# Hybrid decoder trunk: split PSUM tiles, paired chunks and postponed steps in the mixers

## The chip, the cores and the metric

The kernel runs on one core of a Trainium2 chip. The metric is the device time of one execution, in microseconds (us), lower is better. The core has TensorE (PE; PEld are its weight loads), VectorE (DVE), ScalarE (ACT), GpSimd (POOL) and SyncE (SP), which issues the DMAs. Each engine runs its own instructions in the order of the program.

## The reference

One step of a two-layer trunk over 1024 prompt tokens and 32 sample tokens (8 sequences of 4), width 1024, fp32. Cut to what matters:

```python
# layer 0: S5 state space mixer (32 groups of 16 channels, 64 complex states) and retention (4 heads of 128)
bb = f * b                                   # complex product per group: the input matrices of the S5
bu = einsum('blgh,gph->blgp', u, bb);  s = associative_scan(a, bu);  y = Re(c s) + d u
scores = einsum('bihd,bjhd->bhij', q, k) * decay                 # retention, chunk by chunk
o = scores @ v + (q * q_dec) @ s;   s = gamma**c * s + (k * k_dec).T @ v
# layer 1: HGRN2 (8 heads of 128)
scores = where(causal, (q exp(b)) (k exp(-b)).T, 0);  o = scores @ v + (q exp(b)) @ s
s = exp(b_last) * s + (k exp(b_last - b)).T @ v
# both: per-head RMSNorm * silu(gate), output projection, residual, then a gated MLP with a width-3 conv
```

## The kernel before

Activations lie with features on the 128 partitions and tokens along the free axis, cut into three token chunks `CH` of 384, 384 and 288. A dense tile (`dense`, `mm`, `mm1`, L258) multiplies a 1024x128 weight tile with all tokens: for each chunk 8 row blocks times 3 passes (weight and activation are both split into a high and a low fp32r part), 72 matmuls, into one of 4 `acc` PSUM banks. VectorE then empties the bank. The other 4 PSUM banks are the ring `misc`, for all small products of the mixers.

The order of all instructions is made while the program is built. `run_jobs` walks through the dense tiles. `at(dt, fn)` puts a side step on a list with a due time; `tick` moves the clock on by 1/8 after each row block, so that one unit is one token chunk of a dense tile and three units are a tile, and `run_side` emits every side step that has come due. An instruction of a side step thus stands at a fixed place between the matmuls of the dense tiles, whether or not its inputs are there by then: where they are not, TensorE waits in front of it. `flush` emits all that is left. Due times come from the table `P`.

The parts that the change touches:

- Start of layer 0 (`first`): the first two weight tiles run while the S5's constants are worked out on VectorE (`s5_setup`, `s5_inputs`, replayed at L150), then `rms1` puts the logarithms of the mean squares on ScalarE (L338, L340), `finish` puts the exponentials (L348) on it and `rms3`, `rms4` on VectorE (L351 to L355).
- S5 inputs (`s5_x`): for each of 16 pairs of groups, `bst` makes two small input matrices on VectorE (L818 to L821: two products and a sum each, from the tile `bc`, loaded by a DMA for each 4 groups), GpSimd multiplies them with powers (`va`, L843 to L847), TensorE transposes the result (`turn`, L856) and multiplies it with the tokens (`prod`, L865). `s5_within` and `s5_carry` scan over time on VectorE (L880 to L884). `s5_y` makes the outputs; it calls `bst` again for each pair (L818, L819, L823, L824).
- Retention (`retention`): 8 chunks of 128 tokens a head. `first(n)` puts a score product and a transpose into one `misc` bank; VectorE takes the score (`sT`, L1149), ScalarE the transpose (`kt`, L1150), GpSimd makes `qd`. `second(n)`, due `lagA` later, puts the state product (L1161), the output product (L1162) and the product with the old state (L1164) into one bank; VectorE makes the new state `S` (L1169) and ScalarE copies the output (L1170).
- HGRN2 (`hgrn`): per head and token chunk a chain on VectorE (`prep`, `scans`, `base`, `level` three times; L1553 to L1609), its last product `kfin` on GpSimd (L1613). Then for each of 8 chunks `first(nn)` (scores L1652, transpose L1653, products of the levels L1636, all in one bank; ScalarE copies the levels into `sTb`, L1642 and L1645; VectorE adds the diagonal blocks by a predicated copy, L1657; ScalarE copies `kt`, L1659) and `second(nn)` (L1670, L1671, L1673; VectorE `S`, L1676 or L1678; ScalarE the output, L1679).

In both layers a head takes three dense tiles (q, k or f, v), in layer 1 four from the sixth head on (a gate tile), so its side steps lie beside the tiles of the next head.

## Time and profile before

| | us |
|---|---|
| median of 3 runs | 2786.41 (2781.28 to 2787.82) |
| profiled execution, its time | 2786.47 |
| profiled execution, its span | 2784.5 |
| PE busy | 2632.7 (95%) |
| DVE busy | 1623.1 (58%) |
| ACT busy | 978.2 (35%) |
| POOL busy | 780.9 (28%) |

The span goes from the first to the last instruction. Busy shares over the whole span mix stages with different limits; a table by stretch and the list of waits say more. In such a table "PEclk" is the clock granted to TensorE as a share of full speed; in a list of waits a line reads "who waits <- for whom: us in total, times, longest".

### The profile page before, as it was taken

The numbers are of one execution on the slowest core, as the hardware profiler recorded it, in microseconds if no ns is written. First come the engines' busy times: TensorE is split into PE (matmuls) and PEld (weight loads), VectorE is DVE, ScalarE is ACT, GpSimd is POOL, SyncE is SP. The second block draws the span as 40 slices with busy tenths as digits, with TensorE's granted clock in tenths as the row PEclk, the third lists the DMA queues.
The fourth block names the chain that finished last, engine by engine and source line by source line (L and its number), as shares of the span: only waits on it lengthen the run. The fifth ranks groups of instructions, "written<-read, shape, count | busy, mean of one in ns | idle before, by whom it ended". The sixth has DMA issues, their size and how long they took to land.

```text
span 2784.5 us, 42698 instructions
## 1 busy us (share of the span) xinstructions
PE 2632.7 (95%) x16388; PEld 2598.3 (93%) x16388; DVE 1623.1 (58%) x3414; ACT 978.2 (35%) x2120; POOL 780.9 (28%) x1173
## 2 busy tenths in 40 slices
PE   6778998999999999999989999989999999999998
PEld 5768998999999999999988889989999999999998
DVE  8996664565444444445787787765455444444445
ACT  4224444452212121214444445444432222222224
POOL 5636671321101010102434344442211010101013
PEclk8899999999999999999999999999999999999999
DMA  3412224111111111112211111112211111111112
GB/s 120 99 42 64 67 78 136 42 49 46 50 42 50 42 50 42 50 42 76 76 50 47 40 56 47 47 40 77 78 48 46 46 46 46 46 46 46 46 46 88
DMA packets 110539, 159.96 MB, mean 57 GB/s; under 512 B 18944, under 2 KB 48256, under 8 KB 110336
## 3 DMA queue, kind: packets, MB, share of 16 engines
q1 hardware_dynamic: 109760, 156.65, 17.9%
q8 instruction: 129, 2.11, 0.3%
q14 instruction: 74, 0.61, 0.1%
q10 hardware_dynamic: 576, 0.59, 0.1%
HBM read 136.45 MB, written 20.74 MB: 56 GB/s over the span
## 4 chain that ended last, share of the span: by engine, by line
PE 77%; DVE 15%; ACT 3%; issue 2%; POOL 1%; DMA 1%; SPq 1%; DVEq 0%; ACTq 0%; POOLq 0%
PE acc L258 71%; DVE hF L1606 1%; DVE s_t L881 1%; PE misc L1113 1%; DVE s_t L880 1%; DVE s_t L882 1%; DVE rb L351 1%; PE misc L1673 1%; DVE hS L1607 1%; DVE sall L884 0%; DVE lv L1601 0%; DVE sall L883 0%; DVE nsq L355 0%; DVE hR L1580 0%; DMA x<-in_x_dram 0%
## 5 line engine op out<-in xcount | busy, mean ns | idle before, releaser
L258 PE MATMUL acc<-hh,whi 128*128 128x384 f32 (+1 forms) x3320 | 1111.4, 335 | 9.2 <-ACT hh L284 7.0
L258 PE MATMUL acc<-hl,whi 128*128 128x384 f32 (+1 forms) x3320 | 1085.2, 327 | 8.8 <-DVE hl L290 8.8
L258 PE MATMUL acc<-hh,wlo 128*128 128x384 f32 (+1 forms) x3320 | 1084.4, 327 | 0.4 <-POOL wlo L189 0.4
L258 PEld LDWEIGHTS acc<-hl,whi 128*128 128x128 f32 x3320 | 635.8, 192 | 13.6 <-DVE hl L290 11.8
L258 PEld LDWEIGHTS acc<-hh,whi 128*128 128x128 f32 x3320 | 636.7, 192 | 11.0 <-ACT hh L284 7.8
L258 PEld LDWEIGHTS acc<-hh,wlo 128*128 128x128 f32 x3320 | 634.1, 191 | 1.0 <-POOL wlo L189 0.7
L1306 POOL TENSOR_TENSOR sl<-cv,rstd 128x384 f32<-128x384 f32 x132 | 122.0, 924 | 1218.4 <-ACT cv L345 1218.4
L188 ACT ACTIVATE whi<-raw 128x512 fp32r<-128x512 f32 x392 | 239.3, 620 | 394.1 <-PE acc L258 385.4
L189 DVE TENSOR_TENSOR wlo<-raw,whi 128x512 fp32r<-128x512 f32 x298 | 238.9, 802 | 143.9 <-ACT whi L188 141.1
L258 PE MATMUL acc<-hdl,whi 128*128 128x384 f32 (+1 forms) x984 | 318.2, 323 | 0.0
L258 PE MATMUL acc<-hdh,wlo 128*128 128x384 f32 (+1 forms) x984 | 318.2, 323 | 0.0
L258 PE MATMUL acc<-hdh,whi 128*128 128x384 f32 (+1 forms) x984 | 317.8, 323 | 0.0
L1335 DVE TENSOR_TENSOR x<-acc,x 128x384 f32<-128x384 f32 (+1 forms) x264 | 138.3, 524 | 239.4 <-PE acc L258 239.1
L258 PE MATMUL acc<-ys,whi 128*128 128x384 f32 (+1 forms) x768 | 187.8, 330 | 9.8 <-DVE x L617 3.7
L1298 ACT ACTIVATE cv<-ext,vec 128x384 f32<-128x384 f32 x132 | 90.6, 687 | 288.1 <-DVE ext L1286 226.8
L258 PEld LDWEIGHTS acc<-hdh,whi 128*128 128x128 f32 x984 | 185.1, 188 | 0.3
L258 PEld LDWEIGHTS acc<-hdl,whi 128*128 128x128 f32 x984 | 185.1, 188 | 0.3
L258 PEld LDWEIGHTS acc<-hdh,wlo 128*128 128x128 f32 x984 | 185.3, 188 | 0.0
L189 POOL TENSOR_TENSOR wlo<-raw,whi 128x512 fp32r<-128x512 f32 x94 | 127.5, 1358 | 203.7 <-ACT whi L188 202.9
L1300 DVE SCALAR_TENSOR_TENSOR cv<-ext,vec,cv 128x384 f32<-128x384 f32 x132 | 78.0, 591 | 169.2 <-ACT cv L1298 169.2
L282 ACT ACTIVATE hdh<-sl 128x384 fp32r<-128x384 f32 x132 | 65.9, 499 | 247.8 <-DVE sl L1323 247.8
L258 PEld LDWEIGHTS acc<-ys,whi 128*128 128x128 f32 x768 | 136.8, 192 | 12.8 <-DVE x L617 4.0
(379 smaller groups left out, 3636.6 us busy)
## 6 DMA issues: line engine op xcount, KB each, us to landing
raw<-in_w_gate_dram SPq DMA_DIRECT2D x88, 256.0 KB, 2.6
raw<-in_w_up_dram SPq DMA_DIRECT2D x88, 256.0 KB, 2.6
raw<-in_w_dn_dram SPq DMA_DIRECT2D x88, 256.0 KB, 2.6
raw<-in_w_c_dram SPq DMA_DIRECT2D x64, 256.0 KB, 2.7
raw<-in_w_ab_dram SPq DMA_DIRECT2D x40, 256.0 KB, 2.8
x<-in_x_dram SPq DMA_DIRECT2D x15, 528.0 KB, 7.2
ush<-uD SPq DMA_DIRECT2D x128, 34.0 KB, 1.9
xD<-x SPq DMA_DIRECT2D x8, 528.0 KB, 3.2
```

What stands on the lines that cost most here:

```text
L188: nc.scalar.activation(hi[:, s], raw, AF.Copy)
L189: eng.tensor_tensor(lo[:, s], raw, hi[:, s].bitcast(F32), OP.subtract)
L258: self.nc.tensor.matmul(ps[:, :c1 - c0], a[:, o:o + 128], b[:, c0:c1], start=first and p == 0, stop=last and p == 2)
L282: nc.scalar.activation(h, src, AF.Copy)
L351: self.nc.vector.scalar_tensor_tensor(b, b, -0.5, a, OP.mult, OP.mult)
L880: eng.tensor_tensor(t2[hi], s[lo], ms[lo].to_broadcast(half), OP.mult)
L881: eng.tensor_tensor(t2[lo], s[hi], ms[hi].to_broadcast(half), OP.mult)
L882: (eng2 or eng).tensor_tensor(t1, s, mr.to_broadcast(shape), OP.mult)
L1298: nc.scalar.activation(cv[:, :ln], ext[:, 0:ln], AF.Identity, bias=self.v(f"cb{l}", m), scale=cwv(0, m))
L1300: nc.vector.scalar_tensor_tensor(cv[:, :ln], ext[:, 1:ln + 1], cwv(1, m), cv[:, :ln], OP.mult, OP.add)
L1306: nc.gpsimd.tensor_tensor(s[:, :npr], cv[:, :npr], self.rstd[:, c0:c0 + npr], OP.mult)
L1335: nc.vector.tensor_tensor(X[m][:, c0:c1], ps, X[m][:, c0:c1], OP.add)
```

## The change

1. **Separate PSUM tiles.** A `first` now takes two `misc` banks: one that only VectorE reads (scores) and one that only ScalarE reads (transposes, level products). `second` is cut in two: `states` (state products, one bank, VectorE) and `outputs` (one bank, due `lagO` = 0.5 or `lagP` = 0.4 units after).
2. **Chunks in pairs.** One such step serves two chunks: 4 pairs a head in retention, 5 groups of 2 or 1 in HGRN2. In retention the decay matrix is replaced by a row factor (`kinv`) and a triangle in one VectorE instruction, the query decay is put on the output (by VectorE, with the copy out of PSUM), and `qd` on GpSimd goes. In HGRN2 the predicated copy becomes a step of its own (`inner`, due `mid` = 0.25 after).
3. **S5 input matrices at once.** `s5_b`, called once in `first` of layer 0 right after the constants, makes all 32 matrices `b1` by 9 VectorE instructions and their turned copies `b2` by 6 ScalarE instructions, from three DMAs that `s5_load` issues. `bst` goes; in `s5_y` a broadcast copy by ScalarE takes its place. `bc` is loaded for `s5_y` only, at half the size.
4. **Postponed steps.** While the program is built a model (`Ahead`) follows when each engine would finish each instruction and when each tile is ready. `at` takes a list of needed tiles (`need`), a condition (`ok`) and a class (`thr`). A step that is due is held back while its inputs, or the next `misc` bank, are ready by the model more than `slack` = 100 ns later than TensorE (for `inner`: VectorE) would get to it, and so are the later steps of its class. `at` drops all three in phase "A", so it holds from the start of layer 1 on. `require` emits what a tile must have before it may start: in phase "C" a head's q and v tiles wait until the head two before is done, a gate tile until its norm is. `flush` and `require` do not ask the model. At most 3 token chunks of HGRN2 are live (`live`).

The core of the diff (waits and names as in the text; the same `need`/`ok` lists are given to the other steps of the mixers):

```diff
+    def at(self, dt, fn, need=None, ok=None, thr=None):
         self.seq += 1
+        if self.ph == "A":
+            need = ok = thr = None
+        self.side.append([(self.now if self.base is None else self.base) + dt, self.seq, fn, need, ok, thr, False])
...
+    def step(self, until):
+        barred = set()
+        for i, x in enumerate(self.side):
+            t, _, fn, need, ok, thr, _ = x
+            if until is not None and t > until:
+                return False
+            if thr in barred or (ok is not None and not ok()) or (
+                    until is not None and need is not None and self.late(need())):
+                if thr is not None:
+                    barred.add(thr)
+                x[6] = True
+                continue
+            self.side.pop(i)
+            self.base = max(t, self.now) if x[6] else t
+            fn()
+            self.base = None
+            return True
+        return False
+    def late(self, need):
+        ...
+        t = max([a.ready(*need, eng=eng)] + [a.over_with(n) for n in a.ring.get(self.misc_key, [])[:banks]])
+        return t > a.at[eng] + P["slack"]
+    def require(self, done):
+        while self.ph == "C" and not done():
+            assert self.step(None)
...
             play(len(setup))
+            self.s5_b()
             u_work(0)
...
+    def s5_b(self):
+        for g, n in ((0, 12), (12, 12), (24, 8)):
+            ...
+            nc.vector.tensor_tensor(a, B[:, 0], self.fr[:, G, None].to_broadcast([128, n, SH]), OP.mult)
+            nc.vector.tensor_tensor(b, B[:, 1], self.fis[:, G, None].to_broadcast([128, n, SH]), OP.mult)
+            nc.vector.tensor_tensor(self.b1[:, G], a, b, OP.add)
+            nc.scalar.activation(self.b2[0:64, G], self.b1[64:128, G], AF.Copy, scale=-1.0)
+            nc.scalar.activation(self.b2[64:128, G], self.b1[0:64, G], AF.Copy)
...
-            self.bst(bc, g, 2, b1, self.fr, self.fis, False)
-            self.bst(bc, g, 2, b2, self.frs, self.nfi, True)
...
-            self.bst(bc, g, 2, bz3[:, :, 16:144], self.fr, self.fis, False)
+            nc.scalar.activation(bz3[:, :, 16:144].rearrange("p g (r h) -> p g r h", h=2 * SH)[:, :, :, 0:SH],
+                                 self.b1[:, g:g + 2, None, :].to_broadcast([128, 2, 4, SH]), AF.Copy)
...
+        def first(p):                                            # retention
+            ps, pt = self.misc(), self.misc()
+            ...  # two score products into ps, two transposes into pt
+            nc.scalar.activation(kt, by(pt[:, :256]), AF.Copy, scale=self.c("kdec", h))
+            nc.vector.scalar_tensor_tensor(sT, by(ps[:, :256]), self.c("kinv", h),
+                                           self.tri[:, None, :].to_broadcast([128, 2, 128]), OP.mult, OP.mult)
+        def states(p):
+            pk = self.misc()
+            ...  # two state products into pk, then two updates of S on VectorE
+        def outputs(p):
+            po = self.misc()
+            ...  # per chunk the output product and the product with the old state
+            nc.vector.tensor_tensor(by(o[:, 256 * p:256 * p + 256]), by(po[:, :256]),
+                                    qdec[:, None, :].to_broadcast([128, 2, 128]), OP.mult)
...
+        PAIRS = ((0, 0, 2), (0, 2, 1), (1, 0, 2), (1, 2, 1), (2, 0, 2))        # HGRN2
+        def first(g):
+            ps, pt = self.misc(), self.misc()
+            ...  # scores into ps; transposes and level products into pt; ScalarE copies levels and kt
+            def inner():
+                for x in range(m):
+                    V.copy_predicated(sT[:, x], self.mdiag, ps[:, 128 * x:128 * x + 128])
+            self.at(P["mid"], inner, lambda: ("vector", [sT[:, :m]]), None, "rec0")
...
         def qtile(w, R):
+            self.qheads.append(R)
+            self.require(lambda: len(self.qheads) < 3 or self.qheads[-3].get("smp") and self.qheads[-3].get("sec") == 8)
```

## Rows read from the trace of the kernel before

**Rows 1.** Stretches: length, busy PE PEld DVE ACT POOL, PEclk, DMA, GB/s.
```profile
66.00:200.00 134.00, 97.03 (x549) 92.88 (x550) 126.61 (x370) 30.74 (x76) 65.46 (x118) 0.86 0.29 70
200.00:430.00 230.00, 209.85 (x1421) 204.67 (x1420) 153.81 (x387) 105.87 (x276) 148.47 (x239) 0.97 0.24 67
...
1372.00:1672.00 300.00, 271.93 (x1780) 264.73 (x1779) 238.76 (x571) 141.05 (x403) 119.00 (x115) 0.94 0.14 48
1672.00:1870.00 198.00, 177.58 (x1148) 173.27 (x1147) 138.74 (x324) 95.33 (x260) 85.79 (x83) 0.96 0.14 45
...
1950.00:2740.00 790.00, 790.00 (x4899) 789.08 (x4898) 372.75 (x662) 216.71 (x394) 114.80 (x235) 1.00 0.16 50
```

**Rows 2.** Waits of TensorE over the whole span.
```profile
PE misc L1670 <- ACT kt L1659: 27.3, 11, 4.6
PE misc L856 <- POOL va L847: 25.8, 6, 10.1
PE misc L1673 <- DVE S L1676: 16.0, 6, 3.2
PE misc L1161 <- ACT kt L1150: 9.8, 4, 2.7
PE misc L1053 <- DVE vf L1046: 9.1, 3, 4.2
...
PE misc L1164 <- DVE S L1169: 8.7, 6, 3.9
```

**Rows 3.** Waits of all engines, 1372 to 1880 us.
```profile
ACT kt L1659 <- DVE sTb L1657: 81.9, 58, 5.0
DVE sTb L1657 <- ACT sTb L1645: 53.2, 24, 5.3
ACT hy L1679 <- DVE S L1678: 52.8, 30, 4.4
```

**Rows 4.** Instructions in order of time around 1508 us: start, length, engine.
```profile
1508.18 0.29 DVE L1657 COPY_PREDICATED sTb<-mdiag,misc 128x128 f32<-128x128 uint8 x1
...
1508.50 0.28 ACT L1659 ACTIVATE kt<-misc 128x128 f32<-128x128 f32 x1 [4.04 <-DVE sTb L1657]
...
1508.83 0.38 PE L1670 MATMUL misc<-vt,kt 128*128 128x128 f32 x1 [2.37 <-ACT kt L1659]
```

**Rows 5.** Busy time by stretch, one head of layer 1.
```profile
1494.00:1553.30 59.30, 52.37 (x346) 50.95 (x346) 47.74 (x114) 28.98 (x83) 24.29 (x24) 0.94 0.14 46
```

**Rows 6.** Busy time of the instructions that touch the tile `ba` (DVE; L818, L821, L823, L824).
```profile
66.00:160.00 94.00, 14.98 (x64) 0.84 0.38 90
200.00:430.00 230.00, 18.84 (x48) 0.97 0.24 67
```

**Rows 7.** Busy time of the instructions of L819.
```profile
66.00:160.00 94.00, 6.84 (x32) 0.84 0.38 90
200.00:430.00 230.00, 4.02 (x16) 0.97 0.24 67
```

**Rows 8.** Waits of all engines, 66 to 200 us.
```profile
POOL va L843 <- DVE b L821: 24.9, 11, 5.5
```

**Rows 9.** Instructions in order of time at the start, three places.
```profile
50.63 0.58 ACT L338 ACTIVATE sacc<-misc,eps 128x384 f32<-128x384 f32 x1 [4.30 <-PE misc L334]
...
54.31 1.30 ACT L348 ACTIVATE sacc<-sacc 128x384 f32<-128x384 f32 x3
...
57.80 0.18 DVE L150 COPY s_frs<-s_fr 64x32 f32<-64x32 f32 x1
...
58.01 0.56 DVE L351 SCALAR_TENSOR_TENSOR rb<-rb,sacc 128x384 f32<-128x384 f32 x1
...
70.62 0.47 PE L856 MATMUL misc<-ident,va 128*128 128x128 f32 x1 [10.09 <-POOL va L847]
```

**Rows 10.** Groups of instructions, 0 to 500 us: count, busy us, mean ns, idle before.
```profile
L1149 DVE TENSOR_TENSOR sT<-misc,dq 128x128 f32<-128x128 f32 x32 | 9.1, 283 | 3.3 <-PE misc L1146 2.9 <-PE misc L1162 0.2
...
L1170 ACT ACTIVATE yr<-misc 128x128 f32<-128x128 f32 x32 | 8.8, 276 | 38.8 <-DVE S L1169 35.9 <-DVE S L1167 2.8
```

662 lines of the change are left out of this document (454 added, 208 removed).

## The prediction

> **What bounds the kernel now.** I read the busy times by stretch first [rows 1]. In the MLPs TensorE is busy all the time at full clock: 790.00 of 790.00 us in the second one. There nothing changes and nothing can be won. The time that can be won lies where TensorE stands still, or runs at the lower of its two clock levels (1.2 against 2.4 GHz) after having stood still. For a stretch I count its idle time plus (1 - PEclk) times its length. That gives 37.0 + 18.8 = 55.8 us for 66 to 200 (S5 inputs and scans), 20.2 + 6.9 = 27.1 us for 200 to 430 (retention, S5 outputs), 28.1 + 18.0 = 46.1 us for 1372 to 1672 (HGRN2, five heads) and 20.4 + 7.9 = 28.3 us for 1672 to 1870 (its other heads). The reader should see that VectorE is busy 94% from 66 to 200 and 80% from 1372 to 1672, but 67% and 70% in the other two.
>
> Then the list of waits says in front of what TensorE stands [rows 2]. In layer 1: for `kt` 27.3 us and for `S` 16.0 us. In layer 0: for `va` 25.8, `kt` 9.8, `S` 8.7 us, and most of 9.1 for `vf`. Behind these stand waits between ScalarE and VectorE [rows 3]: `kt` waits 81.9 us for the predicated copy, the predicated copy 53.2 us for the level copies, the output copy 52.8 us for `S`. `kt` needs nothing from the predicated copy; both only read the same PSUM bank. One such stall in order of time [rows 4]: VectorE gets to its copy at 1508.18, since its queue is full; `kt` starts at 1508.50, after 4.04 us of idle ScalarE; TensorE goes on at 1508.83, after 2.37 us.
>
> **Layer 1, from 1372 to 1870.** Split banks let `kt` run when its transposes are there, and postponed steps keep TensorE from standing in front of what the model calls late. Neither takes work away: VectorE keeps its 47.74 us a head [rows 5]. TensorE's own floor for that head is 59.30 less 6.93 idle less 0.06 x 59.30 = 48.8 us. Two queues of nearly the same length won't overlap perfectly. I take 53 us a head (VectorE 90% busy) against 60 (300 us are five heads): 5 x 7 = 35. The bounds are 58 (what is late merely moves) and the floor, where all 46.1 us come back. From 1672 to 1870 VectorE has room, and I take two thirds of 28.3: 19; bounds 9 and 28.3. Against it stands `require`. From the third head on, a q tile waits until the head two before is done, and whatever is left is emitted at one place without asking the model. Behind it in TensorE's queue stands the whole next tile. No row shows this wait. It costs nothing if the head is done, and a third of a head's VectorE work, 16 us, if one token chunk is still open. I take 1 us for each of six heads, -6, since a head's steps were due before that point even now. Sum: 48, from about 7 to 74.
>
> **S5 inputs, 66 to 200.** `bst` goes: 14.98 + 6.84 = 21.8 us of VectorE up to 160 [rows 6, 7], an upper bound, as neighbours overlap a little. GpSimd stands 24.9 us for its results [rows 8], and TensorE for `va` behind it. With VectorE at 94% I count three quarters as reaching TensorE: 16, bounds 5 and 22. What is late next is VectorE's scan itself, and the DMA that brings the tokens.
>
> `s5_b` brings back 9 products at about 0.283 us [rows 10], 2.5 us of VectorE, and a new wait at a bad place. Its 6 ScalarE copies stand ahead of the logarithms in ScalarE's queue and wait for VectorE's constants, which are done at 58 us [rows 9]. The logarithms started at 50.63 and can now start at 57.8 + 2.5 + 0.3, about 61. The exponentials started 3.7 us after them and would end their first at about 65.2, so that `rms3` starts there and not at 58.01: 7 us later, and with it the scaling of the tokens, their stores and `va`. TensorE stood until 70.62 for `va`, of which some 2 to 3 us were the wait for `bst` (24.9 us in 11 waits), now gone. I take -5, bounds 0 and -10. The three DMAs of `s5_load` go into SP's queue ahead of later weights; I count nothing, as the first `va` is the later one; if that cover fails, it is inside the same bound.
>
> **Retention and S5 outputs, 200 to 430.** ScalarE no longer waits for VectorE in front of `kt`: of 9.8 us I take back 9. For `S` I take 4 of 8.7: fewer waits, but two updates now run in a row half a unit ahead of the outputs. TensorE's clock gives 3. The 18.84 + 4.02 = 22.9 us that `bst` costs VectorE there [rows 6, 7] are what keeps its queue short. They pay for the output copies that move to VectorE: 16 at most twice 0.283 us each, 9.1 us, against 8.8 us that ScalarE loses [rows 10]. `qd` on GpSimd goes and hides behind other work; ScalarE's broadcast copy for `s5_y` too, as ScalarE is 46% busy. Phase "A" drops all conditions, so due times stay what they were, and a step that comes early still stops TensorE. Sum 16, bounds 4 and 22.
>
> At one place a rule speaks against the change. One copy of 128 columns takes ScalarE 0.276 us and a VectorE instruction 0.283 us [rows 10]; in a pair, what the first chunk's product waits for is done later by one such piece. The Trainium skill (Perfetto Trace Analysis, Optimizing Scalar/DVE Operations) says that where these engines are not saturated but cause bubbles on others, smaller instructions may let work be done sooner. By that rule pairing is the wrong way round; it is a rival below.
>
> **Sum.** 48 + 16 - 5 + 16 = 75 us off the profiled execution's 2786.5 us (its span of 2784.5 and 2 around it): 2711 us. That execution is 0.1 us from the median of the runs, so no correction is made. About 0.3%, or 8 us, can be told from no change.
>
> **The rivals.**
> - *VectorE takes over as the bound of layer 1.* Its order is fixed too, and a faster TensorE only moves the wait to the `acc` banks, which VectorE empties. For it: 47.74 against 48.8 us [rows 5]. Against it: VectorE's own 53.2 us of waiting [rows 3] mostly go. With 57 us a head, 10 us after that, 2 us for each `require` and 10 less in layer 0: 15 + 10 - 12 + 17 = 30 off, 2756 us.
> - *All of it comes back.* 74 in layer 1, 42 in layer 0 (20 + 22): 2670 us. Against it: the start, and the equal queues.
> - *Pairs lengthen the chain.* 40 full pairs (24 in HGRN2, 16 in retention) times 0.276 + 0.283 us [rows 10], if nothing hides it: 22 us less gain, 2733 us. For it: due times don't move with the pairs. Against it: in layer 1 the postponing covers it.
> - *It does not do what it says.* The model's clock and the chip's drift apart, steps are held or let go at the wrong places, and the waits come back under other names; with the late start and VectorE's gain of layer 0 about even: 2784 us.
> - *Slower: `require` emits chains in one piece.* If a held step leaves one token chunk open at each of six q tiles, TensorE stands 16 us [rows 5] each: 96 us, against 54 + 27 won, 15 us slower, 2801 us; with more left, beyond. It decides from 13.5 us a head (81 / 6). For it: postponing delays the end of each head, and classes hold back what stands behind. Against it: VectorE's work fits into a head's time.
>
> **How the numbers follow.** Forecast 0.47 (own range 2690 to 2732), pairs 0.10, VectorE 0.18, all of it 0.08, no effect 0.07, slower 0.10. The likeliest gives 2711 us. From 2670 (all bounds at their best) to 2772 (the VectorE case at its worse end) lie the forecast, the pairs, nearly all of the VectorE case and half of the best one, about 0.78. Faster by over 0.3%: 0.47 + 0.10 + 0.18 + 0.08 = 0.83; within 0.3%: 0.07; slower: 0.10.
>
> **What would show it.** Layer 1: the wait of TensorE for `kt` and `S` gone from the list, heads of about 53 us, PEclk there at 0.97 or more; if heads take 57 or more and TensorE waits in front of `acc`, VectorE bounds. Start: the logarithms at about 61 us, the first transpose of `va` near 75; no later wait for `bst`'s successor. Retention: `kt` starts without waiting for `sT`. The prediction is wrong if layer 1 keeps over 50 us of idle and slow time, if q tiles start after long gaps, or if the start costs over 10 us.

## The result and the profile after

The changed kernel takes 2764.4 us (median of 2761.6 to 2769.1) against 2786.7 us before (2781.3 to 2787.8): ratio 0.9926, 95% interval 0.9907 to 0.9945. 22 us came off where 75 were forecast. The sign was right. The time lies in the wide range (2670 to 2772), outside the forecast's own (2690 to 2732) and nearest to the rival in which VectorE takes over (2756). Less than a third of the gain came, and the runs below show that even these 22 us are not made of what the forecast made them of.

The busy times by stretch of the changed kernel come first (length, busy PE, PEld, DVE, ACT, POOL, PEclk, DMA, GB/s); the first four answer to [rows 1], the fifth is one head of HGRN2 and answers to [rows 5], the last is a piece of the scans in layer 0.

```profile
66.00:200.00 134.00, 98.76 (x567) 95.54 (x568) 126.08 (x300) 31.65 (x75) 72.70 (x121) 0.85 0.27 69
200.00:430.00 230.00, 216.03 (x1467) 211.28 (x1465) 140.75 (x310) 102.71 (x250) 136.28 (x212) 0.97 0.26 72
1372.00:1672.00 300.00, 278.96 (x1826) 269.05 (x1826) 245.47 (x577) 148.41 (x392) 123.82 (x119) 0.98 0.15 48
1672.00:1870.00 198.00, 185.11 (x1192) 179.00 (x1191) 136.30 (x316) 98.75 (x243) 80.81 (x79) 0.97 0.15 48
1485.20:1541.05 55.85, 51.28 (x346) 49.54 (x345) 47.21 (x113) 28.23 (x76) 22.75 (x23) 1.00 0.15 49
154.20:177.30 23.10, 18.29 (x109) 17.93 (x110) 22.09 (x56) 5.98 (x14) 3.75 (x3) 0.85 0.05 13
```

From 1372 to 1672 TensorE stands still 21.0 us instead of 28.1, at PEclk 0.98 instead of 0.94: better, but far from what was forecast. From the first `hq` (the evacuated q) of the third head to that of the sixth, three heads, it takes 172.4 us (1426.51 to 1598.87), before 180.0 (1441.60 to 1621.63): 57.5 us a head instead of 60.0, where I had forecast 53. The fifth line is the useful one: at full clock TensorE is busy for 51.28 us in a head.

The waits of TensorE in layer 1 (1330 to 1890) answer to [rows 2]; in this trace nearly every instruction carries line L208, so they are told apart by tile:

```profile
PE misc L208 <- ACT kt L208: 7.4, 8, 2.1
PE acc L208 <- ACT whi L208: 7.3, 6, 2.1
PE acc L208 <- POOL wlo L208: 7.2, 7, 2.5
PE misc L208 <- DVE S L208: 5.5, 7, 1.7
```

`kt` (27.3) and `S` (16.0) have shrunk as forecast. In their place stand `whi` and `wlo`, the two halves of a converted weight, which before cost TensorE 1.3 us in all of layer 1. How they come about is seen around 1503 us (instructions of four engines in order of time: start, length, in brackets the idle time before):

```profile
1502.58 0.55 DVE L208 TENSOR_TENSOR hz<-acc,rstd 128x384 f32<-128x384 f32 x1
1503.17 0.53 ACT L208 ACTIVATE hz<-hz 128x384 f32<-128x384 f32 x1 [6.64 <-DVE hz L208]
1503.60 0.62 ACT L208 ACTIVATE whi<-raw 128x512 fp32r<-128x512 f32 x1
1504.29 1.42 POOL L208 TENSOR_TENSOR wlo<-raw,whi 128x512 fp32r<-128x512 f32 x1 [0.68 <-ACT whi L208]
...
1505.76 0.44 PE L208 MATMUL acc<-hh,wlo 128*128 128x384 f32 x1 [0.64 <-POOL wlo L208]
```

VectorE is late with the evacuation `hz`. ScalarE stands 6.64 us for it, since the sigmoid is next in its fixed order. The weight conversion stands behind the sigmoid, GpSimd's half behind that, and TensorE at the end of the row. Two groups of waits say how much of it there is, the first from 1372 to 1672, the second from 1672 to 1872; first before, then changed:

```profile
ACT hz L345 <- DVE hz L1469: 6.3, 9, 0.8
...
ACT gt L345 <- DVE gt L1247: 3.0, 6, 1.1
```

```profile
ACT hz L208 <- DVE hz L208: 37.3, 9, 9.1
ACT gt L208 <- DVE gt L208: 45.3, 13, 8.5
```

The 81.9 us that ScalarE stood for the predicated copy [rows 3] are gone, but it now stands for VectorE at these two places, 82.6 us.

To see which stage gained, I take three landmarks in each trace: the first `hq` of layer 1 (all of layer 0 lies ahead of it), the last `ys<-hy` (HGRN2 lies between the two), and the end. After the last `ys` all kernels need 866 to 869 us. In the table "to HGRN2" is the first landmark and "HGRN2" the difference of the two.

| kernel | us | ratio to before (95%) | to HGRN2 | HGRN2 |
|---|---|---|---|---|
| before | 2786.7 | | 1357.4 | 561.1 |
| changed | 2764.4 | 0.9926 (0.9907 to 0.9945) | 1346.6 | 546.7 |
| f3: before + input matrices at once | 2768.9 | 0.9937 (0.9921 to 0.9952) | 1340.5 | 560.9 |
| f1: before + banks apart | 2785.6 | 0.9993 (0.9983 to 1.0003) | 1363.3 | 554.2 |
| g1: f1 with five banks | 2790.7 | 1.0016 (1.0006 to 1.0025) | 1360.9 | 560.7 |
| e1: changed, no holding | 2779.9 | 0.9977 (0.9967 to 0.9987) | 1349.1 | 567.0 |
| g5: e1 with single chunks | 2771.3 | 0.9946 (0.9931 to 0.9960) | 1344.8 | 557.4 |
| e5: changed, retention's banks shared | 2761.5 | 0.9909 (0.9894 to 0.9924) | 1340.9 | 550.2 |
| f2: changed, HGRN2's banks shared | 2747.1 | 0.9856 (0.9839 to 0.9872) | 1345.4 | 531.8 |
| e2: changed, sigmoid and silu later | 2751.4 | 0.9880 (0.9865 to 0.9895) | 1347.5 | 534.9 |
| e7: changed, 1 us of margin | 2748.2 | 0.9860 (0.9845 to 0.9875) | 1344.2 | 535.5 |
| e3: changed, no reciprocals | 2743.7 | 0.9851 (0.9833 to 0.9868) | 1344.6 | 528.4 |
| e4: changed, copies behind the logarithms | 2760.9 | 0.9911 (0.9896 to 0.9926) | 1338.5 | 550.1 |
| e6: changed, S a step of its own | 2766.7 | 0.9927 (0.9912 to 0.9941) | 1345.4 | 551.9 |
| e8: changed, outputs later | 2758.9 | 0.9900 (0.9883 to 0.9916) | 1346.5 | 542.8 |
| c4: e2, e4, e7, e8 together | 2760.3 | 0.9902 (0.9884 to 0.9920) | 1339.6 | 553.7 |
| g4: c4 with three hq | 2765.2 | 0.9922 (0.9906 to 0.9939) | 1339.4 | 557.6 |
| c5: e5, f2, e4 together | 2745.9 | 0.9855 (0.9840 to 0.9869) | 1336.5 | 539.4 |
| c7: c5 + e2 | 2729.2 | 0.9804 (0.9787 to 0.9820) | 1339.3 | 523.5 |
| c8: c5 + conversions earlier | 2746.1 | 0.9864 (0.9849 to 0.9879) | 1335.8 | 541.3 |

The landmarks are of one profiled execution each, so the table itself says how far to trust them. Eight kernels have layer 0 exactly as changed (changed, e1, e2, e3, e6, e7, f2, g5): 1344.2 to 1349.1. Four have HGRN2's code as changed (changed, e4, e5, e8): 542.8 to 550.2. In these four the order is nevertheless not the same, as the model that postpones steps begins layer 1 with other clocks: of 941 VectorE instructions in e8's HGRN2, 825 stand in the order of the changed kernel. In e4 it is 928 of 941, and yet HGRN2 took 3.4 us longer there, so the order is not all of this scatter. A profiled execution can also lie off the median of its kernel, e1's by 4.3 us (2784.2). So under 5 us in layer 0 and under 8 us in HGRN2 I read nothing into a single kernel.

### The profile page after: what moved, and what is told of

It reads as the page before. It is cut to its first block, busy times and chain, and to the rows that moved or that the text cites. A ratio compares the mean times of both kernels' runs of the same rounds, so it can differ in the third digit from the quotient of the medians.

```text
span 2761.6 us, 42451 instructions
## 1 busy us (share of the span) xinstructions
PE 2631.6 (95%) x16388; PEld 2593.2 (94%) x16388; DVE 1603.2 (58%) x3261; ACT 971.7 (35%) x2048; POOL 767.3 (28%) x1144
## 4 chain that ended last, share of the span: by engine, by line
PE 74%; DVE 17%; ACT 3%; issue 2%; DMA 1%; SPq 1%; POOL 1%; DVEq 0%; ACTq 0%; POOLq 0%
PE acc L208 69%; PE misc L208 5%; DVE s_t L208 2%; DVE hR L208 2%; DVE hF L208 1%; DVE hS L208 1%; DVE rb L208 1%; DVE sall L208 1%; DVE lv L208 1%; SPq L208 1%; DVE nsq L208 1%; DVE hy L208 1%; ACT sTb L208 1%; DMA x<-in_x_dram 0%; DVE hl L208 0%
## 5 line engine op out<-in xcount | busy, mean ns | idle before, releaser
L208 PE MATMUL acc<-hh,whi 128*128 128x384 f32 (+1 forms) x3320 | 1101.9, 332 | 16.2 <-ACT hh L208 6.4
L208 PE MATMUL acc<-hl,whi 128*128 128x384 f32 (+1 forms) x3320 | 1081.9, 326 | 8.1 <-DVE hl L208 8.1
L208 PE MATMUL acc<-hh,wlo 128*128 128x384 f32 (+1 forms) x3320 | 1081.5, 326 | 8.0 <-POOL wlo L208 7.2
L208 PEld LDWEIGHTS acc<-hh,whi 128*128 128x128 f32 x3320 | 630.7, 190 | 20.6 <-ACT whi L208 7.7
L208 PEld LDWEIGHTS acc<-hl,whi 128*128 128x128 f32 x3320 | 630.5, 190 | 12.7 <-DVE hl L208 10.8
L208 PEld LDWEIGHTS acc<-hh,wlo 128*128 128x128 f32 x3320 | 629.7, 190 | 10.9 <-POOL wlo L208 9.5
L208 POOL TENSOR_TENSOR sl<-cv,rstd 128x384 f32<-128x384 f32 (+2 forms) x176 | 151.0, 868 | 1219.8 <-ACT cv L208 1219.8
L208 ACT ACTIVATE whi<-raw 128x512 fp32r<-128x512 f32 x392 | 239.0, 620 | 398.1 <-PE acc L208 386.5
L208 DVE TENSOR_TENSOR x<-acc,x 128x384 f32<-128x384 f32 (+1 forms) x360 | 187.6, 523 | 281.1 <-PE acc L208 280.8
L208 DVE TENSOR_TENSOR wlo<-raw,whi 128x512 fp32r<-128x512 f32 x298 | 238.7, 801 | 140.7 <-ACT whi L208 137.8
L208 PE MATMUL acc<-hdl,whi 128*128 128x384 f32 (+1 forms) x984 | 317.9, 323 | 0.0
L208 PE MATMUL acc<-hdh,wlo 128*128 128x384 f32 (+1 forms) x984 | 317.7, 323 | 0.0
L208 PE MATMUL acc<-hdh,whi 128*128 128x384 f32 (+1 forms) x984 | 317.4, 323 | 0.0
L208 DVE SCALAR_TENSOR_TENSOR cv<-ext,vec,cv 128x384 f32<-128x384 f32 (+1 forms) x264 | 156.0, 591 | 173.1 <-ACT cv L208 168.4
L208 PE MATMUL acc<-ys,whi 128*128 128x384 f32 (+1 forms) x768 | 189.7, 333 | 12.5 <-DVE x L208 4.8
L208 ACT ACTIVATE cv<-ext,vec 128x384 f32<-128x384 f32 x132 | 90.7, 687 | 287.9 <-DVE ext L208 226.7
L208 PEld LDWEIGHTS acc<-hdl,whi 128*128 128x128 f32 x984 | 184.9, 188 | 0.3
L208 PEld LDWEIGHTS acc<-hdh,whi 128*128 128x128 f32 x984 | 184.8, 188 | 0.3
L208 PEld LDWEIGHTS acc<-hdh,wlo 128*128 128x128 f32 x984 | 185.0, 188 | 0.0
L208 POOL TENSOR_TENSOR wlo<-raw,whi 128x512 fp32r<-128x512 f32 x98 | 134.0, 1370 | 171.9 <-ACT whi L208 151.0
L208 ACT ACTIVATE hdh<-sl 128x384 fp32r<-128x384 f32 x132 | 65.9, 499 | 249.3 <-DVE sl L208 249.3
L208 PEld LDWEIGHTS acc<-ys,whi 128*128 128x128 f32 x768 | 138.0, 193 | 15.8 <-DVE x L208 5.1
```

The lines of the kernel that those rows point to most:

```text
L208: return fn(*a, **k)
```

## The experiments

### What each part of the change is worth

**f3_inputs_only.** `s5_b`, `s5_load`, the smaller `bc` and ScalarE's broadcast copy, put into the kernel before; nothing else.

```diff
-            self.bst(bc, g, 2, b1, self.fr, self.fis, False)
-            self.bst(bc, g, 2, b2, self.frs, self.nfi, True)
+            (once, ahead of u_work:) self.s5_b()
```

> The kernel before, with one part of the change alone: the state space mixer's input matrices made at once (with the copies for the outputs on ScalarE). Theory (this part is what gained in layer 0: 7.5 us up to the first v tile, and 2 to 4 more in the state space mixer's outputs): about 2776 us (2773 to 2780). Rival (the pairs in retention carry half of layer 0's gain of 11): 2779 to 2784 us, no more than 7.5 off.

Measured: 2768.9 us, 16.6 off, more than either expected. Its first `vf` comes at 154.16 (before 161.71), its last `sT` at 384.98 (401.88), its first `hq` at 1340.5. So the input matrices gain 7.5 us up to the first v tile and 9.4 more in the stretch of retention and the state space mixer's outputs. It is alone worth three quarters of the whole change.

**f1_split_only.** Only the separate banks, in the kernel before.

```diff
-            ps = self.misc()
+            ps, pt = self.misc(), self.misc()
-            nc.tensor.transpose(ps[:, 128:256], k[:, c], self.ident)
+            nc.tensor.transpose(pt[:, 128:256], k[:, c], self.ident)
(and p0 beside p1 in HGRN2)
```

> The kernel before, with one part of the change alone: in retention and in HGRN2 the scores that VectorE reads get a bank of their own beside the transposes and level products that ScalarE reads. No pairs, no postponing, no other S5 inputs. The prediction's step (kt's waits, 27.3 + 9.8 us and more, go and the time comes back): about 2762 us (2755 to 2770). Theory by now (kt came late because VectorE's queue is late; without its bank TensorE goes on and stands for S or sTb of the same queue instead): 2783 us (2778 to 2788), with kt's waits under 8 us and those for S and sTb longer by 20 us or more.

Measured: 2785.6 us, no change. The waits for `kt` went, as the prediction said. The first fence has two of TensorE's stalls in retention in the kernel before, the second the same two places in f1:

```profile
193.74 0.49 PE L1161 MATMUL misc<-vt,kt 128*128 128x128 f32 x2 [2.09 <-ACT kt L1150]
...
206.65 0.49 PE L1161 MATMUL misc<-vt,kt 128*128 128x128 f32 x2 [2.61 <-ACT kt L1150]
```

```profile
192.55 0.49 PE L1161 MATMUL misc<-vt,kt 128*128 128x128 f32 x2 [2.13 <-DVE sT L1149]
...
205.36 0.76 PE L1161 MATMUL misc<-vt,kt 128*128 128x128 f32 x2 [2.51 <-DVE sT L1149]
```

Same instruction, same place, same length, another name. This product doesn't read `sT` at all. It may be waiting for the PSUM bank that VectorE has yet to empty, as each chunk now takes one more of the four banks in the ring `misc`. That would make it a question of banks, which the next run asks.

**g1_split_5banks.** f1 with one bank moved from the projections to `misc`.

```diff
-ACC = 4
+ACC = 3
```

> The kernel before with the scores in a bank of their own, as in f1_split_only, and the eight PSUM banks divided 3 to 5 instead of 4 to 4 between the projections' sums and everything else. Theory (the split brought nothing because each chunk now takes one more of four banks, and TensorE stands in front of a bank that VectorE has not emptied: the waits for sT at the state products, for vt at the scores, 10 us between 184 and 441 and 18 us in layer 1): half of these go, about 2772 us (2766 to 2778). Rival (the order of work behind VectorE sets the pace, banks or not; or three banks are too few for the projections): 2781 to 2795 us.

Measured: 2790.7 us; the theory of the bank ring falls. TensorE's waits in retention (184 to 441):

```profile
PE misc L1162 <- DVE sT L1149: 6.5, 3, 2.5
PE misc L1164 <- DVE S L1169: 6.0, 4, 3.9
...
PE misc L1161 <- DVE sT L1149: 0.8, 1, 0.8
```

With a fifth bank the state product (L1161) goes, and the very next product (L1162), which does read `sT`, stands there for it. VectorE is late at that place whatever bank it reads; `kt` was only the first to show it. In layer 1 the names changed likewise: from f1 to g1 TensorE's waits for `vt` fall from 10.5 to 3.0 us and those for `kt` rise from 1.5 to 7.7. (The projections pay too: one wait of 6.5 us in front of `hq` with three banks, 2.3 with four. That a gain of a few us hides behind this is not ruled out.) The Trainium skill (Perfetto Trace Analysis, Matmuls) advises to rotate independent matmul groups through different banks so that evacuation overlaps; here neither one bank more per chunk nor a fifth bank gained, since the groups are not independent of VectorE for longer than one product.

**e1_no_hold.** The changed kernel without postponing.

```diff
-        return t > a.at[eng] + P["slack"]
+        return False
```

> The changed kernel, but no step is ever held back because the model says that its operands are late: every step is emitted at its due time, the conditions on earlier steps stay. Theory (postponing is what shortened layer 1): TensorE again stands in front of what is late, some 10 of the 14 to 16 us that layer 1 gained are lost, about 2775 us (2770 to 2781), with TensorE's waits for S, kt and sTb back by that much between 1330 and 1750. Rival (the separate banks and the pairs shortened it, postponing only moves waits about): 2764 us give or take 4.

Measured: 2779.9 us. Postponing is worth 15.5 us, more than expected. Without it HGRN2 takes 567.0 us (in an execution 4.3 us above the median), no shorter than before the change. TensorE's waits from 1330 to 1672, one of the four equal stalls, and what VectorE did there:

```profile
PE misc L208 <- DVE S L208: 32.3, 5, 7.6
```

```profile
1503.51 0.28 DVE L208 COPY S<-misc 128x128 f32<-128x128 f32 x1
1503.83 0.35 DVE L208 SCALAR_TENSOR_TENSOR S<-S,hF,misc 128x128 f32<-128x128 f32 x1
```

```profile
1503.85 0.80 PE L208 MATMUL misc<-hR,S 128*128 128x128 f32 x2 [7.63 <-DVE S L208]
```

Before, TensorE stood 27.3 us for `kt` and 16.8 for `S` in layer 1. Now it is 1.6 for `kt` and 32.3 + 13.1 for `S` in the two halves: 44.1 us have become 47.0. With f3 this gives the sum of the change: inputs -16.6 (2785.5 to 2768.9), pairs, banks and conditions +11.0 (to 2779.9), postponing -15.5 (to 2764.4).

**g5_singles.** e1 with eight single chunks in HGRN2.

```diff
-        PAIRS = ((0, 0, 2), (0, 2, 1), (1, 0, 2), (1, 2, 1), (2, 0, 2))
+        PAIRS = tuple((n // 3, n % 3, 1) for n in range(8))
```

> The changed kernel without holding steps back, as in e1_no_hold, and with single chunks instead of pairs in HGRN2 (the separate banks stay; three sTb tiles). Theory (a pair puts two updates of S and four operations of ScalarE between a product and what it waits for, and TensorE's 45.4 us of waits for S there come from this): S waits of 25 us or less and about 2767 us (2762 to 2772). Rival (the pairs cost nothing, the conditions and the bank ring do): 2776 to 2785 us.

Measured: 2771.3 us, 8.7 less than e1, with 3.2 us of waits for `S` in layer 1 instead of 45.4; waits for `hy` (16.6) and `sTb` (13.4) took part of the place. So without postponing the pairs do lengthen the chain, as the rival of that name said, by some 9 us in HGRN2; that is little more than the scatter, but the waits for `S` are clear. It agrees with the rule of the Trainium skill (Perfetto Trace Analysis, Optimizing Scalar/DVE Operations) by which smaller instructions may help where these engines hold up others. Single chunks together with postponing were not tried; whether the pairs cost anything there is open.

**e5_shared** and **f2_hg_shared.** The changed kernel with scores and transposes in one bank again, first in retention, then in HGRN2. ScalarE's copy is emitted ahead of VectorE's, as in the changed kernel and unlike before.

```diff
-            ps, pt = self.misc(), self.misc()
+            ps = self.misc()
+            pt = ps[:, 256:512]
(e5; in f2 only the transposes move to ps[:, 256:512], the level products stay in pt)
```

> The changed kernel, but in retention the transposes of k go back into the bank of the scores (columns 256 to 511), so that ScalarE and VectorE read one bank again; pairs and all due times as changed. Theory (the separate tiles took 14.5 us of waits for kt out of TensorE's list between 185 and 441, and the pairs gave 4.6 of that back as longer waits for S): waits for kt of 8 to 15 us come back, the last head's scores stand some 6 to 10 us later, about 2771 us (2768 to 2775). Rival (these waits hide under others in retention): 2764 us give or take 3.

> The changed kernel, but in HGRN2 the transposes go back into the scores' bank (columns 256 to 511), which VectorE's predicated copy reads; the level products stay apart. Theory (with postponing the model keeps TensorE off what is late, whatever bank it is in, so the separate bank is worth little): 2764 to 2771 us. Rival (the separate bank is what lets postponing work): kt's waits of 15 us or more come back and the kernel takes 2778 us or more.

Measured: e5 2761.5 us, f2 2747.1 us; both are no slower, f2 17 us faster. Neither theory had that. In e5 layer 0 ends at 1340.9, below all eight kernels with separate banks (1344.2 to 1349.1), and as f3 without pairs (1340.5); in f1 the banks alone put it from 1357.4 to 1363.3. Each of these differences is near the scatter of 5 us. With the copies of e4 moved, sharing brings less: 1338.5 with separate banks (e4), 1336.5, 1339.3 and 1335.8 with shared ones (c5, c7, c8). So the separate banks of retention gain nothing; that they cost something is not shown. Nor do its pairs gain: in f3, without them, TensorE stands 13.2 us for `kt` and 1.0 for `S` between 170 and 441, in e5 none for `kt` and 12.9 for `S`, 7.1 of them in one wait. In HGRN2 f2 needs 531.8 us, 11 less than the best of the four with separate banks. Why sharing doesn't hurt is in the waits between the two engines, in retention (170 to 441) before and in e5, then in HGRN2 (1330 to 1890) in f2:

```profile
ACT kt L1150 <- DVE sT L1149: 45.8, 20, 6.7
```

```profile
DVE sT L208 <- ACT kt L208: 5.3, 5, 2.3
```

```profile
DVE sTb L208 <- ACT kt L208: 1.3, 3, 0.5
```

Where VectorE's reader was emitted first, ScalarE's `kt` waited 45.8 us for `sT` in retention and 81.9 us for the predicated copy in HGRN2 [rows 3], as VectorE's queue was late. With the order turned round VectorE waits 5.3 and 1.3 us for `kt`. In retention no step is postponed, so there it isn't the model that does this. What the shared bank cost looks like the order of its two readers. These kernels differ from the one before in more than that (the pairs, and in HGRN2 the postponing); the turned order alone, in the kernel before, was not run.

### Where layer 1's time is

**e2_luts_later.**

```diff
-                self.lut(z[:, :c1 - c0], z[:, :c1 - c0], AF.Sigmoid)
+                def sig():
+                    self.lut(z[:, :n], z[:, :n], AF.Sigmoid)
+                    R.setdefault("zs", set()).add(ci)
+                self.at(0.25, sig, lambda: ("scalar", [z[:, :n]]))
(the same for the silu of a gate in layer 1; prep waits for ci in R["zs"])
```

> The changed kernel, but in HGRN2 the sigmoid of an f tile and the silu of a gate are steps of their own, emitted a quarter of a unit later and only when the model says that VectorE has delivered their input. Theory (ScalarE's queue stands behind VectorE, the weight conversions stand behind that, and TensorE waits for weights, 16 us in layer 1): ScalarE's waits for hz and gt from VectorE (37.3 + 12.6 and 45.3 us) shrink to a third, TensorE's waits for whi and wlo fall from 16 to under 4 us, and the kernel takes about 2753 us (2748 to 2758). Rival (VectorE's work bounds the heads): the waits move in front of S, hq or acc and the time stays within 2761 to 2767.

Measured: 2751.4 us, as the theory said. TensorE's waits for weights from 1330 to 1950 fall from 16.1 (5.7 + 2.7 for `wlo` and `whi` to 1672, 4.6 + 1.6 + 1.5 behind it) to 2.0 us, ScalarE's for `gt` behind 1672 from 45.3 to 12.4. But the gain comes where VectorE has room: from the seventh head's first `hq` to the last `ys` it is 200.7 us (1681.62 to 1882.36) against 216.5 in the changed kernel (1676.87 to 1893.35), while the five heads ahead of it need no less than there (1376.73 to 1681.62, 304.9, against 302.5), with a new wait of TensorE there:

```profile
PE misc L208 <- POOL hz L208: 11.7, 2, 5.9
```

**e3_light.**

```diff
-            V.reciprocal(Re, Se)
-            V.reciprocal(Ro, Fo)
+            V.tensor_copy(Re, Se)
+            V.tensor_copy(Ro, Fo)
```

> The changed kernel with the reciprocals in HGRN2's base step replaced by copies (left out: the reciprocal itself, some 7.6 us of VectorE per head become about 1.6). Rival (VectorE's work bounds a head of layer 1): nearly all of 6 us a head comes off, until TensorE's 51.3 us a head is reached: heads of 52 to 53 us instead of 57.5, 35 to 45 us in all, about 2725 us. Theory (no engine is the bound, but the fixed orders of the queues against one another): VectorE catches up sooner, yet only a third of it reaches TensorE, heads of about 55.5 us, about 2748 us (2742 to 2756).

Measured: 2743.7 us. I had put the saving at 6 us a head; the groups of instructions (1330 to 1900: count, busy us, mean ns, idle before) say less, first the changed kernel, then e3:

```profile
L208 DVE RECIPROCAL hR<-hS 128x192 f32<-128x192 f32 x16 | 21.5, 1345 | 0.1
L208 DVE RECIPROCAL hR<-hF 128x192 f32<-128x192 f32 x16 | 20.7, 1294 | 0.0
```

```profile
L208 DVE COPY hR<-hS 128x192 f32<-128x192 f32 x16 | 11.6, 725 | 0.1
L208 DVE COPY hR<-hF 128x192 f32<-128x192 f32 x16 | 9.9, 620 | 0.0
```

With the three smaller forms it is 59.7 us against 28.5: 31.2 us less VectorE work, 3.9 a head. The third to fifth head take 55.6 us each (1422.94 to 1589.68) instead of 57.5, as the theory said, and the time is in its range. So in these heads about half of what is taken from VectorE reaches the end, although it is busy only 82% there (245.47 of 300 us). HGRN2 as a whole became 18.3 us shorter, but that is not all VectorE's: 8.7 of it lie in the seventh head (68.9 to 60.2 us from first `hq` to first `hq`), and in f2, where nothing is taken from VectorE, that head takes 60.2 us too.

**e7_margin.**

```diff
-P = {"slack": 100.0,
+P = {"slack": -1000.0,
```

> The changed kernel, but a step is held until its operands have been ready for 1 us by the model, not only until they are at most 0.1 us late. Theory (what TensorE still waits for in layer 1, apart from weights, are small misses of the model, 0.3 to 2.5 us each, S, kt, hq, hT and sst together some 18 us): most of these go, about 2757 us (2752 to 2761). Rival (holding longer only puts the chains of the heads later, and they end in the steps that must be out before the next tile, or ScalarE and VectorE then stand longer for TensorE): 2763 to 2775 us.

Measured: 2748.2 us, less than even the theory's best; HGRN2 535.5. Holding steps longer costs nothing here. But the theory's reason is not what the trace shows: the waits it named, `S`, `kt`, `hq`, `hT` and `sst`, fall only from 18.3 to 14.4 us between 1330 and 1890 (`kt` from 7.4 to 7.1), those for weights from 16.0 to 11.5, and one of 3.2 for `hz` is new. The gain lies mostly in the sixth head, which takes 65.8 us instead of 78.0 from its first `hq` to the next; why there is open.

**e6_s_later.**

```diff
+            def update():
                 SS[g] = [] ... S2 ... R["S"] = S2
+            self.at(0.1, update, lambda: ("vector", [pk[:, :128 * m]]), None, "rec3")
```

> The changed kernel, but in HGRN2 the two state updates S of VectorE are a step of their own behind the products, emitted only when the model says that VectorE would find the products done. Theory (VectorE stands 31.0 + 21.7 us in front of S for TensorE, and what is queued behind it comes late): that waiting falls under 15 us and 5 to 10 us come off, about 2757 us (2753 to 2760). Rival (VectorE is ahead of TensorE when it stands there, so the time is spare, and the outputs only get S later): 2762 to 2770 us, with TensorE's wait for S longer than the 5.6 us that it has there now.

Measured: 2766.7 us, in the rival's range; the 2.3 us to the changed kernel are within the scatter. VectorE's waits for `S` (31.0 us) are gone from its list, and it stands for `sst` 14.9, `sTs` 13.1, `vf` 11.1 and `hz` 10.9 us instead (1330 to 1672). So that waiting was mostly spare time, as the rival said. Its sign, a longer wait of TensorE for `S`, did not come (2.6 us against 5.5, 1330 to 1890); the waits for weights grew instead, from 16.0 to 22.7.

### The start and retention's outputs

**e4_start.**

```diff
             G = slice(g, g + n)
             ...
-            nc.scalar.activation(self.b2[0:64, G], self.b1[64:128, G], AF.Copy, scale=-1.0)
-            nc.scalar.activation(self.b2[64:128, G], self.b1[0:64, G], AF.Copy)
(moved into finish(), behind the copies of u)
```

> The changed kernel, but the six ScalarE copies of the state space mixer's input matrices stand behind the exponentials and the copies of u instead of ahead of the logarithms. Theory (they cost the start what was put down as -5): the logarithms start at 50 to 51 us instead of 58.40, the first transpose of va at 68 to 70 instead of 74.48, and 3 to 5 us of that are left at the end: about 2760 us. Rival (VectorE, busy over 90% from 66 to 200, takes it back): the first vf of the first head is no earlier and the time is 2763 to 2766.

Measured: 2760.9 us. ScalarE's order and the first `va` product, first in the changed kernel, then in e4:

```profile
54.78 0.74 ACT L208 ACTIVATE b<-b 64x192 f32<-64x192 f32 x2 [9.42 <-DVE b L208]
...
58.40 0.58 ACT L208 ACTIVATE sacc<-misc,eps 128x384 f32<-128x384 f32 x1
...
74.48 0.69 PE L208 MATMUL misc<-ident,va 128*128 128x128 f32 x2 [9.61 <-POOL va L208]
```

```profile
48.90 0.58 ACT L208 ACTIVATE sacc<-misc,eps 128x384 f32<-128x384 f32 x1 [2.92 <-PE misc L208]
54.46 0.58 ACT L208 ACTIVATE rb<-misc,eps 128x384 f32<-128x384 f32 x1 [4.98 <-DVE ba L208]
...
60.09 2.13 ACT L208 ACTIVATE b<-b 64x192 f32<-64x192 f32 x6
70.10 0.69 PE L208 MATMUL misc<-ident,va 128*128 128x128 f32 x2 [10.07 <-POOL va L208]
```

The first logarithm comes 9.5 us earlier, but the second waits 4.98 us for VectorE's `ba`, so that the exponentials come only 4.4 us earlier (57.67 against 62.08). The first product is 4.4 us earlier, the first `vf` 3.5 (150.66 against 154.20), the kernel 3.5. In the profiled executions layer 0 ends 8.1 us earlier and HGRN2 takes 3.4 longer, so the last of these agreements is in part luck.

**e8_lagO.** `"lagO": 0.5` becomes 1.0.

> The changed kernel, but in retention the outputs of a pair follow the state products by 1.0 unit instead of 0.5. Theory (the pair made two updates in a row that the first output waits for, and half a unit is too short for it: 13.3 us of TensorE's waits for S between 177 and 430): that wait falls to 6 us or less and 4 to 8 us come off, about 2758 us (2755 to 2761). Rival (the state space mixer's outputs or VectorE's queue take the place): 2762 to 2767 us.

Measured: 2758.9 us, in the theory's range, and yet the theory fell. The wait for `S` is still 11.6 us between 177 and 430, the last `sT` comes at 386.45 (386.24 in the changed kernel), layer 0 is no shorter. The time came in HGRN2, whose code is the same, 542.8 against 546.7: within the scatter of its order. The longest of these waits, 7.1 us at 185.64 in the changed kernel, begins at 178.54: VectorE, busy 22.09 of 23.10 us up to 177.30 (last line of the first fence), is still at the scans and gets to `S` at 185.30.

### Together

**c4** and **g4_c4_hq3.** e2, e4, e7 and e8 in one kernel; then the same with `bufs=3` for `hq` (and 22 scratch tiles for 23), so that a q tile waits for the head three before.

> The changed kernel with four edits together: sigmoid and silu of HGRN2 as steps of their own (alone 13 us), the input matrices' copies behind the exponentials (3.5), steps held until their operands have been ready for 1 us (16), retention's outputs 1.0 unit behind the state products (5.5). If they add, 2726 us; since the first and the third both cut what TensorE waits for in layer 1, I expect them to share a third: 2735 us (2728 to 2743). Over 2745 would say that VectorE's queue sets the pace once the small waits are gone.

> The kernel c4 with three buffers for hq instead of two (and one scratch tile less), so that a q tile waits only for the head three before, and no step has to be emitted by force ahead of it (in c4 30, 3 and 18 steps of the first three such heads were). Theory (c4 lost there: TensorE stood 11.5 and 5.2 us in front of hz, in one piece, behind forced steps): these two waits go, about 2744 us (2738 to 2750). Rival (the luck of the order): the time stays above 2754 us.

Measured: 2760.3 and 2765.2 us; the gains do not add, and neither expectation held. In c4 TensorE stands for `hz` (1330 to 1672):

```profile
PE misc L208 <- POOL hz L208: 16.6, 2, 11.5
```

I took this for the work of `require`, which in c4 emits 30, 3 and 18 steps by force ahead of three q tiles (in the changed kernel 3, 3 and 6; counted while the program is built, no trace shows it). With three buffers no step is forced and this wait is gone, but the time isn't: 14.1 us of waits for `vt`, one of 10.0 us, stand in its place. That forced steps cost c4 its gain is not shown.

**c5**, **c7**, **c8.** c5 is the changed kernel with both banks shared (e5, f2) and e4. c7 adds e2. c8 adds, instead, earlier conversions:

```diff
-                for t in (0.7, 1.1):
+                for t in ((0.4, 0.8) if self.ph == "C" and len(td) == 2 else (0.7, 1.1)):
```

> The changed kernel without separate tiles: in retention and in HGRN2 scores and transposes share a bank again, ScalarE's copy being emitted first, and the input matrices' copies stand behind the exponentials. Theory (the bank that the split adds to each step costs 5.7 us in retention and some 8 to 15 in HGRN2, the start 3.5): about 2740 us (2734 to 2746). Rival (f2_hg_shared had a lucky order): layer 1 takes 547 us as in the changed kernel, about 2753 us.

> The kernel c5 with sigmoid and silu of HGRN2 as steps of their own, as in e2_luts_later. Theory (in c5 TensorE waits 18.4 us for weights in layer 1, since their conversions stand behind ScalarE's waits for VectorE): weights' waits under 4 us, about 2735 us (2730 to 2741). Rival (the steps that come later put the ends of the heads later, as in c4: 20 steps are forced ahead of one q tile, and TensorE stands in front of hz there): 2742 to 2756 us.

> The kernel c5 with the two conversions of a weight 0.4 and 0.8 units after its predecessor's start in layer 1 and behind it, instead of 0.7 and 1.1, so that both stand ahead of the first sigmoid in ScalarE's queue. Theory: the waits for weights, 18.4 us in layer 1, fall to 6 us or less and nothing is put later for it, about 2736 us (2731 to 2741). Rival (ScalarE then waits for the raw weights' transfer, or the waits move to S and hz): 2742 to 2752 us.

Measured: c5 2745.9, between its theory and its rival: of f2's 15 us in HGRN2 7 came again (539.4), so that half of f2's gain may have been its order. c7 2729.2 us, ratio 0.9804, a little better than its theory and the best kernel of this study: some 55 us off the kernel before (2784.7 us in the same round of runs). c8 2746.1 us, on the rival's side. TensorE's waits in layer 1 (1330 to 1890), first c7, then c8:

```profile
PE misc L208 <- DVE S L208: 5.3, 7, 1.6
...
PE misc L208 <- POOL hz L208: 3.6, 1, 3.6
...
PE acc L208 <- ACT whi L208: 2.6, 3, 1.2
```

```profile
PE misc L208 <- POOL hz L208: 15.1, 2, 7.6
...
PE acc L208 <- ACT whi L208: 3.6, 3, 1.6
```

In both the waits for weights fell from c5's 18.4 us to about 6 or less. In c7 nothing large came in their place, in c8 `hz` did. Why there and not in c7 I can't say.

## Why the prediction was wrong, step by step

The largest miss is in layer 1: the step that failed is "I take 53 us a head (VectorE 90% busy) against 60 (300 us are five heads): 5 x 7 = 35." The heads took 57.5 us, 2.5 less instead of 7. In layer 0 it is "of 9.8 us I take back 9", for `kt` in retention. Behind both stands the same error: a wait for `kt` was counted as won when its name would go, while VectorE stayed as late. In retention, and in layer 1 without postponing (e1), TensorE then stood for `sT` and `S` of the same queue. With postponing it stood less, but 16 us for weights whose conversions were held up behind VectorE's evacuations; moving the sigmoid and silu gave 13 us back (e2).

**The start (-5): right.** The logarithms were forecast at 61 and came at 58.40, the first `va` at 75 and came at 74.48; undoing it gives 3.5 us (e4).

**S5 inputs (16): inside its bounds, but half of the gain came elsewhere.** Up to the first `vf` the whole change gains 7.5 us, with the start's 4 some 11, below 16 and inside 5 to 22. What I missed is the second half: the VectorE time that `bst` had cost from 200 to 430 I gave away to the output copies. Alone (f3) it brought 9.4 us there.

**Retention (16): the step that failed is "ScalarE no longer waits for VectorE in front of `kt`: of 9.8 us I take back 9."** The waits went and the time stayed, as TensorE met VectorE's lateness one product later (f1, g1). For `S` I took 4 of 8.7 us back; it grew to 13.3. Layer 0 gained 10.8 us where its inputs alone gain 16.9, so this part gave nothing of its 16 and by these landmarks cost some 6 us, little more than their scatter. Whether the banks or the pairs cost them is not shown.

**Layer 1 (48): 14.4 came.** Four things were mis-sized or missing. My own sign, over 50 us of idle and slow time left, did not show it: by the same count 27.0 + 18.8 = 45.9 us of 74.4 are left from 1372 to 1870. But that window is fixed in time, and as the kernel runs ahead more work falls into it (3018 matmuls against 2928).
- The floor. I took TensorE's floor as busy time less (1 - PEclk) of the whole length, 48.8 us. That charges the slow clock to idle time as well. The changed kernel's head at PEclk 1.00 has 51.28 us.
- "Split banks let `kt` run": worth nothing (f1), and perhaps negative once steps are postponed (f2, c5).
- "Postponed steps keep TensorE from standing in front of what the model calls late": true, and alone worth 15.5 us (e1), some 9 of which make good what the pairs cost (g5).
- Where a stall goes, what is late next: the rival named the `acc` banks. It was the weights: 16 us, by way of ScalarE's queue, which I had not followed past `kt`. The 19 us from 1672 to 1870 were there, but from the seventh head's start to the last `ys` the change gained only 1.3 of them (217.8 to 216.5); e2 gets 15.8 more.

**`require` (-6):** no long gap in front of a q tile; in the changed kernel 3, 3 and 6 steps are forced. It cost nothing that I can see, so this term looks too large; no run leaves `require` out.

**The rivals.** "VectorE takes over" had the nearest time (2756) and more truth than its chance of 0.18: the heads took 57.5 us where it had 57, and about half of what e3 takes from VectorE reaches the end. Its sign, waits in front of `acc` for VectorE's evacuation, was the wrong one to look for; they are passed on through ScalarE and GpSimd. "Pairs lengthen the chain" was right in mechanism (9 us in HGRN2 without postponing, against 22 as upper end), hidden by postponing in the changed kernel. "It does not do what it says" had a part of the mechanism, waits that come back under other names. Of "slower by `require`" nothing was seen in the changed kernel.

**What stays open.** Which part of HGRN2's remaining 5 to 7 us a head above TensorE's 51.3 is VectorE's length and which the order; and why edits that shorten HGRN2 by 11 to 15 us each (e2, e7, f2) add in c7 (e2 and f2) and not in c4 (e2 and e7). The seventh head takes 60 to 62 us in e2, e3, f2 and c7 and 64 to 72 in all others but g4 (88); no run says why.

## What to carry to other kernels

When a wait is taken away, look at what the waiting engine does next: if the following instruction needs the same late engine, the wait changes its name and nothing else (`kt` became `sT`, then `S`). Before a shared bank is split, try turning the order of its two readers, so that the engine with the shorter queue comes first; it costs no bank, though no run here tries it alone. And where an order is written out in advance, an instruction that waits for a late engine should not stand ahead of one on which a third engine depends, as the sigmoid stood ahead of the weights.

## What the runs showed that I had not expected

The same HGRN2 code took 542.8, 546.7, 550.1 and 550.2 us in four kernels that differ only in layer 0. In part the order that came out differed, in part the executions did (e4, with nearly the same order, took 3.4 us longer than the changed kernel). A single edit of layer 1 that gains under 8 us is not told apart from that.

VectorE's instructions at the start are of two lengths. In the changed kernel from 61 to 69 us, GpSimd's and VectorE's in order of time:

```profile
61.78 2.81 POOL L208 TENSOR_TENSOR wlo<-raw,whi 128x512 fp32r<-128x512 f32 x2 [19.23 <-ACT whi L208]
...
63.50 1.51 DVE L208 TENSOR_TENSOR rb<-rb,sacc 128x384 f32<-128x384 f32 x1
65.04 0.56 DVE L208 SCALAR_TENSOR_TENSOR rstd<-rb,sacc 128x384 f32<-128x384 f32 x1
...
65.68 2.86 POOL L208 TENSOR_TENSOR us<-us,rstd 128x384 f32<-128x384 f32 x2 [1.09 <-DVE rstd L208]
...
67.55 1.41 DVE L208 SCALAR_TENSOR_TENSOR rstd<-rb,sacc 128x384 f32<-128x384 f32 x1
```

The same instruction, `rstd` on 128x384, takes VectorE 0.56 us in GpSimd's gap (64.6 to 65.7) and 1.41 us beside a GpSimd instruction. The Trainium skill (Perfetto Trace Analysis, Optimizing Scalar/DVE Operations) says that the two share a read port; the trace agrees, at 0.9 us for this instruction, and here it stands on the path to the first tokens. Not every instruction is hit. Of VectorE's operations on two tensors of 128x384 in the changed kernel, 40 read SBUF alone and lie beside GpSimd over nearly their whole length: 29 of them take over 0.65 us, up to 1.64, where 384 without GpSimd take at most 0.62. Of 39 others that read a PSUM bank beside GpSimd, none takes longer than its like without it.
